# Group statistics taken out of a recurrence's chain, its copies a step later, a new table of a round's pieces, and another split of the query rotation

## The chip, the cores and the metric

The kernel runs on one core of a Trainium2 chip. The metric is device microseconds of one execution. Names of engines: PE is TensorE's matmul, PEld its weight load, DVE is VectorE, ACT is ScalarE, POOL is GpSimd, SP is SyncE.

## The reference, cut to what matters

A first block (convolution and attention, then a feed-forward part) is followed by a two-layer second block over 528 tokens (16 learned ones ahead of 512). Its first layer is a recurrence with 32 heads of 64, its second is an attention with 16 heads. What the change touches is the recurrence with its normalisation over each head's 64 values, and the rotation of the queries:

```python
def _wkv7_scan(r, decay, k, v, a_vec, b_vec):
    ...
    def step(S, inp):
        r_t, w_t, k_t, v_t, a_t, b_t = inp
        sa = jnp.einsum('bhij,bhj->bhi', S, a_t)
        S = S * w_t[:, :, None, :] + sa[..., None] * b_t[:, :, None, :] + v_t[..., None] * k_t[:, :, None, :]
        return S, jnp.einsum('bhij,bhj->bhi', S, r_t)
    ...
    y = _wkv7_scan(r, decay, k, v, -kk, kk * a.astype(jnp.float32))
    mean = jnp.mean(y, axis=-1, keepdims=True)
    var = jnp.mean(jnp.square(y - mean), axis=-1, keepdims=True)
    y = ((y - mean) * lax.rsqrt(var + GN_EPS)).reshape(B, L, D_INNER)

def _rope(x, pos):
    ...
    x1, x2 = xf[..., :half], xf[..., half:]
    return jnp.concatenate([x1 * cos - x2 * sin, x2 * cos + x1 * sin], axis=-1).astype(x.dtype)
```

## The kernel before, in words

All products are made in fp32 from parts: an operand is split into a high part (a copy by ScalarE, `whi`, `qnh`, `knh`) and a low part (a subtraction by GpSimd or VectorE, `wlo`, `qnl`, `knl`), and three matmuls replace one.

The program has three stages: the first block up to about 840 us, the recurrence with the projections that feed it up to about 1900 us, and the attention heads with the output projection to the end.

The recurrence takes the 32 heads in 16 pairs (`Pair`). A pair has 9 chunks (16 tokens, then 8 of 64), and `chain()` takes them one after the other in three steps each. Step one: a bank of PSUM z gets the state's part (L2282) and the mask product's part (L2284), and ScalarE copies it to Z. Step two: z by the inverse R (L2289), and ScalarE's VU. Step three: z by AY and KT (L2294, L2297), from which VectorE makes the next state S (L2301, or L2303 for the first chunk), copies the output to yt or y0 (L1920), and takes the statistics of that output with bn_stats, once for each of the two heads (L2311, L2307). The banks of z are two to a pair and two pairs are in work at once, so a chunk's bank is needed again by the same chain two chunks later, and at a chain's start by the pair after next.

A round begins with a new pair's first z. It holds 15 steps of the new pair and 12 of the old one, in the order MAIN, 27 in all. Between two steps `weave()` pulls pieces of other streams, one piece for a letter, by the table PLAN (L1804, a string of letters for each step): O operands of the pair two ahead, B inverses of its 16 x 16 blocks, L and X the inverse of the pair one ahead and its merge, F rates and K keys of the pair three ahead, M transposes, P the split of weights, R and V loads, and Q `post()` of the pair two behind. Instructions stand on their engine's queue in the order in which they are pulled, so the table sets the order of the work on all engines. All these streams but the keys share one ring of three PSUM banks ("t"), used in turn.

Pieces that the prediction speaks of. Keys: a bank pk of its own with 24 matmuls, pulled two by two (L2009), then a copy kx (L1920). Operands: ScalarE's squares and kk (L1915), GpSimd's kp, the norm n (L2035, L2036) with VectorE's nv, GpSimd's AR (L2052) and kb, VectorE's bd (L2059), kk (L2062) and rk (L2072), a product of two arrays in SBUF; then four groups n of eight matmuls (L2085), each with two VectorE products AN and AY that read its bank (L2089, L2090). Merge: a level y (L2219), then r and t, and so on. Weights: ScalarE's whi in two halves and GpSimd's wlo (L1941). Post: VectorE's short operations on the statistics (L2326 to L2331), GpSimd's power, the normalisation by ScalarE and GpSimd, transposes yT, and a store.

In the heads `Heads` weaves one head's attention with the projections of the next and with parts of the output projection. Evictions of a bank are put down with due times, counted in TensorE's columns (`later`, the table W), and forced when a bank or an operand is needed (`need`, `bank`); the banks "mm" are a ring of three. `p_r` (L1185) rotates the queries of two heads, so it runs eight times. VectorE makes the product with the cosines, rt, from the bank ar, and four products of 32 partitions with the sines, ru, also from ar (L1193), and adds them (L1198); for each head ScalarE makes the high part qr (L1201) and GpSimd the low one (L1202). qnh and qnl (L1172, L1171) empty the bank an of the queries' other part, knh and knl that of the keys, and `last` is a tile of transposed probabilities.

Of the kernel before, what the change touches and what calls it, by code (L numbers as in the profile page):

```python
# [15 lines left out]
P = 128  # L16
S = 512
# [886 lines left out]
SCB = 2  # L904
PTB = 2
LAG = 1.0
ROPE = "dpd"
SCALE = "dpdd"
W = dict(max=2200, exp=100, tot=1400, scale=200, hi=400, lo=150, r0=1700, r1=900, r2=1100, z0=1900, z1=1300)
KS = [0, 16, 144, 272, 400]  # L910
KN = [16, 128, 128, 128, 128]
POF = [0, 144, 416, 816]
# [175 lines left out]
class Heads(Late):  # L1088
# [96 lines left out]
    def p_r(s, h, w):  # L1185

        nc, tp = s.nc, s.tp
        key = ("r", h // 2)
        pp = s.bank("mm", key, MM)
        yield from s.mm3(pp, wv(w, 4, 256)(P), s.CQ)  # L1190
        t1, t2 = (tp.tile([P, S], F32, tag=tg, name=f"{tg}{h}", bufs=1) for tg in ("rt", "ru"))
        c, sn = s.tab[:, 0], s.tab[:, 1]
        pr = lambda o, x, t: nc.vector.scalar_tensor_tensor(o, pp[x], SC, t[x], ALU.mult, ALU.mult)  # L1193
        e = [nc.vector if x == "d" else nc.gpsimd for x in ROPE]
        q4 = [slice(32 * i, 32 * i + 32) for i in range(4)]
        ops = [(0, lambda: pr(t1, slice(None), c))]
        ops += [(0, lambda i=i: pr(t2[q4[i ^ 1]], q4[i], sn)) for i in range(4)]
        ops += [(W["r0"], lambda: e[0].tensor_tensor(t1, t1, t2, ALU.add))]  # L1198
        for b, r in enumerate(HS):
            qr = s.x[h + b, "r"] = tp.tile([P, S], F32R, tag="qr", name=f"qr{h + b}", bufs=4)  # L1200
            ops += [(W["r1"], lambda qr=qr, r=r: nc.scalar.activation(qr[r], t1[r], AF.Copy)),  # L1201
                    (W["r2"], lambda qr=qr, r=r, o=HS[1 - b]: e[1].tensor_tensor(qr[o], t1[r], qr[r].bitcast(F32), ALU.subtract))]  # L1202
        s.later(key, *ops)

    def p_k(s, h, w, i=0):
# [142 lines left out]
    def values(s, h, j):  # L1348
        nc, tp, k = s.nc, s.tp, s.k
        vs, vh, vl = s.v[h // 2]  # L1350
        c = ct(h % 2)
        s.need(("t", h, j), ("v", h | 1, j))
        th, tl = s.pt[j]
        if j == 0:
            s.po = s.bank("po", ("z", h), 1)
            nc.tensor.matmul(s.po, lhsT=vs[:96, c], rhs=th[:96], start=True, stop=False)
            return 512
        a = min((j - 1) * P, 256)
        for i, (x, y) in enumerate(((vh, th), (vl, th), (vh, tl))):
            nc.tensor.matmul(s.po[:, a:], lhsT=x[:, j - 1, c], rhs=y[:, :S - a], start=False, stop=j == 4 and i == 2)  # L1360
        if j == 4:
            s.z[h] = zh, zl = [tp.tile([P, S], F32R, tag="z" + x, name=f"z{x}{h}", bufs=6) for x in "hl"]
            z = tp.tile([P, S], F32, tag="az", name=f"az{h}", bufs=1)
            po = s.po
            s.later(("z", h), (0, lambda: nc.vector.scalar_tensor_tensor(z, po, 0.5, s.sg[h], ALU.mult, ALU.mult)),
                    (W["z0"], lambda: nc.scalar.activation(zh, z, AF.Copy)),
                    (W["z1"], lambda: (nc.vector if ROPE[2] == "d" else nc.gpsimd).tensor_tensor(zl, z, zh.bitcast(F32), ALU.subtract)))
        return 3 * (S - a)


# [430 lines left out]

PLAN = ("OMOKO", "OMOOM", "OOO", "ML", "KO", "OMPOM", "KPO", "OPOO", "OMOKKQ", "XMX", "KOB", "XQK", "QQKO", "XKQKK", "MKXBQX", "KXXOB", "OMBB", "KQXK", "KB", "BVBKF", "XFOQKFQXQ", "KFQXX", "BKXQF", "FKKX", "BFOKBKQ", "RBBFMB", "KKOXBXKB")  # L1804

# [64 lines left out]
class Pair:  # L1872
# [387 lines left out]
    def chain(s):  # L2260
# [5 lines left out]
        for c in range(NC_):  # L2266
# [15 lines left out]
                mm(z[:, :P], lhsT=s.AR[:, c - 1], rhs=S, start=True, stop=False)  # L2282
            for h, q in enumerate(HS):
                mm(z[u, q], lhsT=AK[o, hw[h]] if c else AK[o, h, :], rhs=VU[o, q], start=c == 0 and h == 0, stop=h == 1)  # L2284
            Z = T_("Z" + "ab"[p % 2], (P, P), bufs=2)
            s.ev("Z", Z[u], z[u, :P])
            yield
# [7 lines left out]
            if c < NC_ - 1:  # L2295
                for q in HS:
                    mm(z[q, 2 * P:2 * P + 64], lhsT=KT[:, q], rhs=VU[:, q], start=True, stop=True)  # L2297

                for q in HS:
                    if c:  # L2300
                        nc.vector.scalar_tensor_tensor(Sn[q, q], S[q, q], s.wc[q, c - 1:c], z[q, 2 * P:2 * P + 64], ALU.mult, ALU.add)  # L2301
                    else:
                        nc.vector.tensor_copy(Sn[q, q], z[q, 2 * P:2 * P + 64])  # L2303
            if c == 0:
                s.ev("y0", s.y0, z[:16, :P])
                for h, q in enumerate(HS):
                    nc.vector.bn_stats(s.st[:16, 8 + h, :], z[:16, q])  # L2307
            else:
                s.ev("yt", s.yt[o, j, :], z[o, :P])
                for h, q in enumerate(HS):  # L2310
                    nc.vector.bn_stats(s.st[o, 2 * j + h, :], z[o, q])  # L2311
            yield

    def post(s):
# [8 lines left out]
        var = T_("var", (P, 10))  # L2323
        dm = T_("dm", (P, 10))
        me, mo = st[:, :, 1], st[:, :, 4]
        nc.vector.tensor_tensor(dm, me, mo, ALU.subtract)  # L2326
        nc.vector.tensor_tensor(var, st[:, :, 2], st[:, :, 5], ALU.add)
        nc.vector.tensor_tensor(dm, dm, dm, ALU.mult)
# [60 lines left out]
```

## Time and profile before

| | us |
|---|---|
| median of 3 runs | 2497.18 |
| lowest and highest of them | 2495.27, 2511.31 |
| the profiled execution | 2500.02 |
| its span | 2498.2 |
| TensorE busy in it | 2307.1 |

The rows further down are of that one execution. In a row of a timeline the first number is the start in microseconds, the second the time in the instruction (or in several, with "x4"), and a bracket at its end says how long the engine had stood idle before it and which instruction ended that. A row of waits gives the engine, the line that waited, what it waited for, the sum, the number of times and the longest one. In a row of windows PEclk is TensorE's granted clock as a share of full speed.

### The profile page before, as it was taken

The page shows a single profiled execution, that of the slowest core. Times are in us where ns is not written, and L with a number is a line of the kernel's source. Part 1 is how long each engine was busy: PE and PEld are TensorE (multiplying, and loading weights), DVE is VectorE, ACT ScalarE, POOL GpSimd, SP SyncE. Part 2 cuts the span into 40 slices and gives each one's busy share as a digit, 9 for nine tenths or more (in the row PEclk, how much of TensorE's full clock was granted, in tenths as well). Part 3 has the DMA queues.
Part 4 walks back from the last instruction along what each step waited for, and adds up shares of the span by engine and source line. Part 5 has one row for each costly group of instructions (what it writes and reads, how often), then busy time and mean ns, then how long its engine had stood idle before and what let it go on. Part 6 is the DMA issues. An engine that isn't in the chain of part 4 may idle for free. (4 is left out here: it accounts for less than half of the span.)

```text
span 2498.2 us, 42030 instructions
## 1 busy us (share of the span) xinstructions
PE 2307.1 (92%) x16446; PEld 1976.8 (79%) x16446; DVE 1356.9 (54%) x2956; ACT 991.5 (40%) x2292; POOL 1231.3 (49%) x1431
## 2 busy tenths in 40 slices
PE   7999999999998999898999999999988799999996
PEld 5888888878887999886777777777768587887885
DVE  6762236725746450325677767776333632766665
ACT  5553333423434342222434344444332322554442
POOL 5244555646755663535555455555333634434333
PEclk9999999999998999997999888997889799999998
DMA  3113222223233332322222222223223332111212
GB/s 127 68 68 136 89 97 85 91 92 109 87 112 129 120 120 100 114 97 67 56 59 73 58 63 55 58 64 92 76 67 102 134 110 95 63 65 62 70 52 95
DMA packets 135494, 217.01 MB, mean 87 GB/s; under 512 B 60864, under 2 KB 85888, under 8 KB 125056
## 3 DMA queue, kind: packets, MB, share of 16 engines
q1 hardware_dynamic: 123168, 191.63, 23.7%
q10 hardware_dynamic: 12128, 22.70, 2.4%
q8 instruction: 129, 2.11, 0.3%
q14 instruction: 69, 0.57, 0.1%
HBM read 179.28 MB, written 35.00 MB: 86 GB/s over the span
## 5 line engine op out<-in xcount | busy, mean ns | idle before, releaser
L261 POOL TENSOR_TENSOR wlo<-wraw,whi 128x512 fp32r<-128x512 f32 (+1 forms) x312 | 440.2, 1440 | 333.1 <-ACT whi L260 333.0
L941 POOL TENSOR_TENSOR wlo<-wraw,whi 128x512 fp32r<-128x512 f32 (+2 forms) x207 | 253.9, 1240 | 321.9 <-ACT whi L940 314.3
L260 ACT ACTIVATE whi<-wraw 128x512 fp32r<-128x512 f32 (+1 forms) x312 | 175.3, 615 | 253.3 <-issue 80.4
L940 ACT ACTIVATE whi<-wraw 128x512 fp32r<-128x512 f32 (+2 forms) x207 | 115.3, 590 | 65.5 <-PE p_o_t L1713 20.4
L269 PE MATMUL pu<-f_xh,whi 128*128 128x512 f32 x336 | 131.1, 390 | 0.0
L271 PE MATMUL pu<-f_xh,wlo 128*128 128x512 f32 x336 | 130.7, 389 | 0.0
L270 PE MATMUL pu<-f_xl,whi 128*128 128x512 f32 x336 | 130.7, 389 | 0.0
L1915 ACT ACTIVATE VU<-z,fix_nv 64x64 f32<-64x64 f32 x256 | 64.7, 301 | 161.1 <-PE z L2289 160.4
L2301 DVE SCALAR_TENSOR_TENSOR fix_S<-fix_S,wc,z 64x64 f32<-64x64 f32 x224 | 62.4, 279 | 78.8 <-PE z L2297 45.7
L2009 PE MATMUL pk<-lh_k,whi 128*128 128x264 f32 x256 | 88.1, 344 | 5.6 <-DVE kx L1920 5.6
L2009 PE MATMUL pk<-ll_k,whi 128*128 128x264 f32 x256 | 87.3, 341 | 0.0
L2085 PE MATMUL n<-AR,fix_kb 64*128 64x128 f32 x512 | 74.9, 338 | 13.1 <-DVE AYa L2090 6.8
L1305 POOL COPY ap<-apr 128x96 f32<-128x96 f32 x64 | 16.9, 264 | 141.9 <-DVE apr L1302 102.0
L2009 PE MATMUL pk<-lh_k,wlo 128*128 128x264 f32 x256 | 86.4, 338 | 0.0
L2136 POOL TENSOR_TENSOR t<-n,r 66x14 f32<-66x14 f32 (+6 forms) x224 | 74.0, 330 | 16.2
L2085 PEld LDWEIGHTS n<-AR,fix_kb 64*128 64x128 f32 x512 | 66.9, 236 | 18.3 <-issue 9.4
L1599 PE MATMUL p_g<-lh_g,wlo 128*128 128x264 f32 x256 | 74.9, 292 | 2.6 <-POOL wlo L941 2.5
L2282 PE MATMUL z<-fix_S,AR 128*128 128x128 f32 x256 | 60.3, 321 | 17.6 <-DVE fix_S L2303 11.6
L1599 PE MATMUL p_g<-lh_g,whi 128*128 128x264 f32 x256 | 76.2, 298 | 0.0
L1599 PE MATMUL p_g<-ll_g,whi 128*128 128x264 f32 x256 | 74.3, 290 | 0.0
L816 DVE SCALAR_TENSOR_TENSOR ab<-z,vecs,ab 128x511 f32<-128x511 f32 x44 | 55.6, 1264 | 33.7 <-ACT ab L815 33.7
L270 PEld LDWEIGHTS pu<-f_xl,whi 128*128 128x128 f32 x336 | 63.1, 188 | 13.4 <-issue 0.2
(846 smaller groups left out, 7522.6 us busy)
## 6 DMA issues: line engine op xcount, KB each, us to landing
wraw<-in_w_up_dram SPq DMA_DIRECT2D x22, 1024.0 KB
wraw<-in_w_dn_dram SPq DMA_DIRECT2D x16, 704.0 KB
wraw<-in_a_h_dram SPq DMA_DIRECT2D x16, 640.0 KB
wraw<-in_l_k_dram SPq DMA_DIRECT2D x16, 576.0 KB
wraw<-in_w_gt_dram SPq DMA_DIRECT2D x8, 1024.0 KB
wraw<-in_l_v_dram SPq DMA_DIRECT2D x8, 1024.0 KB
wraw<-in_l_r_dram SPq DMA_DIRECT2D x8, 1024.0 KB
wraw<-in_l_g_dram SPq DMA_DIRECT2D x16, 512.0 KB
```

What stands on the lines that cost most here:

```text
L260: nc.scalar.activation(hi[:p, o], raw[:p, o], AF.Copy)
L261: nc.gpsimd.tensor_tensor(lo[:p, o], raw[:p, o], hi[:p, o].bitcast(F32), ALU.subtract)
L269: nc.tensor.matmul(out, lhsT=wh, rhs=xh, start=start and k == 0, stop=False)
L270: nc.tensor.matmul(out, lhsT=wh, rhs=xl, start=False, stop=False)
L271: nc.tensor.matmul(out, lhsT=wl, rhs=xh, start=False, stop=stop and k == n - 1)
L940: nc.scalar.activation(hi[:, o], raw[:, o], AF.Copy)
L941: nc.gpsimd.tensor_tensor(lo[:, o], raw[:, o], hi[:, o].bitcast(F32), ALU.subtract)
L1599: nc.tensor.matmul(b[:, :HL], lhsT=a, rhs=c[:, o], start=kk == 0 and n == 0, stop=kk == KB - 1 and n == 2)
L1915: s.nc.scalar.activation(out, x, AF.Copy if bias is None else AF.Identity, **({} if scale is None else {"scale": scale}), **({} if bias is ...
L2009: s.nc.tensor.matmul(b_[:, :HL], lhsT=a, rhs=b[:, o], start=i == 0 and q == 0, stop=i == n - 1 and q == 2)
L2085: mm(b_[:, ct((c - 1) % 4)], lhsT=kb[HS[h], c], rhs=s.AR[HS[h], c - 1], start=True, stop=True)
L2136: g.tensor_tensor(tmp[:, :q, :m], n16[:, :q, q:q + 1].to_broadcast([66, q, m]), r16[:, q:q + 1, q + 1:].to_broadcast([66, q, m]), ALU.mult)
```

## The change

The statistics leave `chain()`; `post()` takes them from yt and y0 in SBUF, in five new pieces ahead of its other work, two bn_stats each, on all 128 partitions for the four tiles of yt and on 16 for y0. The copy to yt or y0 of a chunk is put off (`late`) to the next chunk's first step, behind its matmuls; that of the last chunk stays. PLAN gets another order, with 17 Q in place of 13. In `p_r` ScalarE copies the bank ar to rs, scaled; GpSimd makes the product with the cosines and the sum, VectorE the four products with the sines from rs; the due times become other ones. The constant ROPE goes; zl, which it also ruled, stays on VectorE.

```diff
@@ -904,9 +904,8 @@
 SCB = 2
 PTB = 2
 LAG = 1.0
-ROPE = "dpd"
 SCALE = "dpdd"
-W = dict(max=2200, exp=100, tot=1400, scale=200, hi=400, lo=150, r0=1700, r1=900, r2=1100, z0=1900, z1=1300)
+W = dict(max=2200, exp=100, tot=1400, scale=200, hi=400, lo=150, rot=900, z0=1900, z1=1300)
 KS = [0, 16, 144, 272, 400]
 KN = [16, 128, 128, 128, 128]
 POF = [0, 144, 416, 816]
@@ -1188,18 +1187,17 @@
         key = ("r", h // 2)
         pp = s.bank("mm", key, MM)
         yield from s.mm3(pp, wv(w, 4, 256)(P), s.CQ)
-        t1, t2 = (tp.tile([P, S], F32, tag=tg, name=f"{tg}{h}", bufs=1) for tg in ("rt", "ru"))
+        t0, t1, t2 = (tp.tile([P, S], F32, tag=tg, name=f"{tg}{h}", bufs=1) for tg in ("rs", "rt", "ru"))
         c, sn = s.tab[:, 0], s.tab[:, 1]
-        pr = lambda o, x, t: nc.vector.scalar_tensor_tensor(o, pp[x], SC, t[x], ALU.mult, ALU.mult)
-        e = [nc.vector if x == "d" else nc.gpsimd for x in ROPE]
         q4 = [slice(32 * i, 32 * i + 32) for i in range(4)]
-        ops = [(0, lambda: pr(t1, slice(None), c))]
-        ops += [(0, lambda i=i: pr(t2[q4[i ^ 1]], q4[i], sn)) for i in range(4)]
-        ops += [(W["r0"], lambda: e[0].tensor_tensor(t1, t1, t2, ALU.add))]
+        ops = [(W["hi"], lambda: nc.scalar.activation(t0, pp, AF.Copy, scale=SC)),
+               (1500, lambda: nc.gpsimd.tensor_tensor(t1, t0, c, ALU.mult))]
+        ops += [(W["rot"], lambda i=i: nc.vector.tensor_tensor(t2[q4[i ^ 1]], t0[q4[i]], sn[q4[i]], ALU.mult)) for i in range(4)]
+        ops += [(W["rot"], lambda: nc.gpsimd.tensor_tensor(t1, t1, t2, ALU.add))]
         for b, r in enumerate(HS):
             qr = s.x[h + b, "r"] = tp.tile([P, S], F32R, tag="qr", name=f"qr{h + b}", bufs=4)
-            ops += [(W["r1"], lambda qr=qr, r=r: nc.scalar.activation(qr[r], t1[r], AF.Copy)),
-                    (W["r2"], lambda qr=qr, r=r, o=HS[1 - b]: e[1].tensor_tensor(qr[o], t1[r], qr[r].bitcast(F32), ALU.subtract))]
+            ops += [(0 if b else 2500, lambda qr=qr, r=r: nc.scalar.activation(qr[r], t1[r], AF.Copy)),
+                    (1500, lambda qr=qr, r=r, o=HS[1 - b]: nc.gpsimd.tensor_tensor(qr[o], t1[r], qr[r].bitcast(F32), ALU.subtract))]
         s.later(key, *ops)
 
     def p_k(s, h, w, i=0):
@@ -1364,7 +1362,7 @@
             po = s.po
             s.later(("z", h), (0, lambda: nc.vector.scalar_tensor_tensor(z, po, 0.5, s.sg[h], ALU.mult, ALU.mult)),
                     (W["z0"], lambda: nc.scalar.activation(zh, z, AF.Copy)),
-                    (W["z1"], lambda: (nc.vector if ROPE[2] == "d" else nc.gpsimd).tensor_tensor(zl, z, zh.bitcast(F32), ALU.subtract)))
+                    (W["z1"], lambda: nc.vector.tensor_tensor(zl, z, zh.bitcast(F32), ALU.subtract)))
         return 3 * (S - a)
 
 
@@ -1801,7 +1799,7 @@
 
 
 
-PLAN = ("OMOKO", "OMOOM", "OOO", "ML", "KO", "OMPOM", "KPO", "OPOO", "OMOKKQ", "XMX", "KOB", "XQK", "QQKO", "XKQKK", "MKXBQX", "KXXOB", "OMBB", "KQXK", "KB", "BVBKF", "XFOQKFQXQ", "KFQXX", "BKXQF", "FKKX", "BFOKBKQ", "RBBFMB", "KKOXBXKB")
+PLAN = ("OKOMOO", "OMOOM", "OO", "ML", "KQ", "OMPOQ", "KMPOQ", "OPOOXQO", "OMOKKQQ", "M", "XXKOB", "XQK", "QQKO", "XKQKK", "MKXBQX", "KXXOB", "OMKBB", "KQX", "KBB", "BVBKF", "XFOQKFQXQ", "KFQXX", "BKXFKK", "FQ", "BFOKBKQ", "RBBFMB", "KKOXBXKB")
 
 
 
@@ -2282,6 +2280,8 @@
                 mm(z[:, :P], lhsT=s.AR[:, c - 1], rhs=S, start=True, stop=False)
             for h, q in enumerate(HS):
                 mm(z[u, q], lhsT=AK[o, hw[h]] if c else AK[o, h, :], rhs=VU[o, q], start=c == 0 and h == 0, stop=h == 1)
+            if c:
+                late()
             Z = T_("Z" + "ab"[p % 2], (P, P), bufs=2)
             s.ev("Z", Z[u], z[u, :P])
             yield
@@ -2301,14 +2301,13 @@
                         nc.vector.scalar_tensor_tensor(Sn[q, q], S[q, q], s.wc[q, c - 1:c], z[q, 2 * P:2 * P + 64], ALU.mult, ALU.add)
                     else:
                         nc.vector.tensor_copy(Sn[q, q], z[q, 2 * P:2 * P + 64])
+
             if c == 0:
-                s.ev("y0", s.y0, z[:16, :P])
-                for h, q in enumerate(HS):
-                    nc.vector.bn_stats(s.st[:16, 8 + h, :], z[:16, q])
+                late = lambda z=z: s.ev("y0", s.y0, z[:16, :P])
             else:
-                s.ev("yt", s.yt[o, j, :], z[o, :P])
-                for h, q in enumerate(HS):
-                    nc.vector.bn_stats(s.st[o, 2 * j + h, :], z[o, q])
+                late = lambda z=z, o=o, j=j: s.ev("yt", s.yt[o, j, :], z[o, :P])
+            if c == NC_ - 1:
+                late()
             yield
 
     def post(s):
@@ -2323,6 +2322,13 @@
         var = T_("var", (P, 10))
         dm = T_("dm", (P, 10))
         me, mo = st[:, :, 1], st[:, :, 4]
+        for j in range(5):
+            for h, q in enumerate(HS):
+                if j < 4:
+                    nc.vector.bn_stats(st[:, 2 * j + h, :], yt[:, j, q])
+                else:
+                    nc.vector.bn_stats(st[:16, 8 + h, :], s.y0[:, q])
+            yield
         nc.vector.tensor_tensor(dm, me, mo, ALU.subtract)
         nc.vector.tensor_tensor(var, st[:, :, 2], st[:, :, 5], ALU.add)
         nc.vector.tensor_tensor(dm, dm, dm, ALU.mult)
```

The change has two lines fewer ahead of the chain, so a line such as L2301 is the same in both there, while those ahead of it are two lower and those of post six higher.

VectorE in the round of pair 7, from the old pair's yt to the first AN (z_6 and z_7 are the two pairs, bon and rk of pairs 8 and 9, n_9 the groups of pair 9). Before:

```order
L1920 COPY yt_12980<-z_6_13570 64x128
L2311 BN_STATS fix_st_7991<-z_6_13570 64x6 x2
L2201 TENSOR_TENSOR bon_13665<-vP_13419,bo_8_13661 128x264
L2201 TENSOR_TENSOR bon_13665<-vP_13419,bo_8_13662 128x264
L2072 SCALAR_TENSOR_TENSOR rk_13671<-rP_13518,vecs,kp_13494 128x528
L2089 TENSOR_TENSOR AN_13596<-n_9_13685,AN_13596 128x4x64
```

Of the change, from the two bon to the first AN:

```order
L2199 TENSOR_TENSOR bon_13596<-vP_13358,bo_8_13592 128x264
L2199 TENSOR_TENSOR bon_13596<-vP_13358,bo_8_13593 128x264
L2328 BN_STATS fix_st_7993<-yt_12362 128x6 x2
L1918 COPY y_7_13477<-z_7_13478 16x128
L2070 SCALAR_TENSOR_TENSOR rk_13617<-rP_13454,vecs,kp_13436 128x528
L2328 BN_STATS fix_st_7993<-yt_12362 128x6 x2
L1918 COPY yt_12919<-z_6_13511 64x128
L2087 TENSOR_TENSOR AN_13522<-n_9_13630,AN_13522 128x4x64
L2088 TENSOR_TENSOR AYa_13628<-n_9_13630,cst_r 128x4x64
```

Between rk and AN stand now two bn_stats of pair 5 and the old pair's yt copy, and two more bn_stats stand ahead of rk.

TensorE in the same round, the four groups of n_9 and what lies between them (pk of pair 10, y_8 the merge's first level of pair 8). Before:

```order
L2085 MATMUL n_9_13685<-AR_13598,fix_kb_7981 128x128 x4
L2282 MATMUL z_6_13690<-fix_S_7970,AR_11903 128x128
L2284 MATMUL z_6_13690<-VU_12427,AN_11901 64x64 x2
L2085 MATMUL n_9_13698<-AR_13598,fix_kb_7981 128x128 x4
L2085 MATMUL n_9_13705<-AR_13598,fix_kb_7981 128x128 x4
L2085 MATMUL n_9_13712<-AR_13598,fix_kb_7981 128x128 x4
L2289 MATMUL z_7_13673<-Zb_13677,R_13063 64x64 x2
```

Of the change:

```order
L2280 MATMUL z_6_13621<-fix_S_7970,AR_11859 128x128
L2282 MATMUL z_6_13621<-VU_12379,AN_11851 64x64 x2
L2083 MATMUL n_9_13630<-AR_13530,fix_kb_7981 128x128 x4
L2083 MATMUL n_9_13637<-AR_13530,fix_kb_7981 128x128 x4
L2083 MATMUL n_9_13644<-AR_13530,fix_kb_7981 128x128 x4
L2217 MATMUL y_8_13651<-Tm_13562,AN_12965 64x64 x8
L2083 MATMUL n_9_13663<-AR_13530,fix_kb_7981 128x128 x4
L2289 MATMUL z_7_13606<-Zb_13611,R_13003 64x64 x2
```

The old pair's z moved ahead of the first group, and a level y ahead of the fourth.

ScalarE at the fifth rotation (rs, qr of heads 8 and 9, qnh of the bank an, knh of the bank ak). Before:

```order
L1172 ACTIVATE p_6_21988<-at_0_21983 96x512
L940 ACTIVATE whi_21974<-wraw_21710 128x512
L1201 ACTIVATE qr_21994<-rt_21992 64x512
L1201 ACTIVATE qr_21995<-rt_21992 64x512
L1172 ACTIVATE qnh_21996<-an_22000 128x512
L1172 ACTIVATE knh_22026<-ak_1_22028 128x264
L1172 ACTIVATE knh_22026<-ak_0_22037 128x264
```

Of the change:

```order
L1171 ACTIVATE p_6_21868<-at_0_21863 96x512
L939 ACTIVATE whi_21854<-wraw_21590 128x512
L1193 ACTIVATE rs_21872<-ar_21831 128x512
L1171 ACTIVATE qnh_21877<-an_21881 128x512
L1199 ACTIVATE qr_21875<-rt_21873 64x512
L1199 ACTIVATE qr_21876<-rt_21873 64x512
L1171 ACTIVATE knh_21903<-ak_1_21905 128x264
L1171 ACTIVATE knh_21903<-ak_0_21919 128x264
```

qnh stands now ahead of qr, behind rs; knh is still behind qr.

## Rows read from the trace of the kernel before

**Rows 1.** The page's first lines, us busy, share of the span and instructions

```profile
span 2498.2 us, 42030 instructions
PE 2307.1 (92%) x16446; PEld 1976.8 (79%) x16446; DVE 1356.9 (54%) x2956; ACT 991.5 (40%) x2292; POOL 1231.3 (49%) x1431
```

**Rows 2.** Windows, three rounds: us, busy PE PEld DVE ACT POOL, PEclk, DMA share, GB/s

```profile
1408.40:1451.30 42.90, 39.83 (x452) 32.60 (x453) 31.81 (x98) 18.16 (x53) 23.41 (x44) 0.92 0.25 64
1451.30:1499.70 48.40, 45.63 (x452) 37.28 (x453) 31.66 (x98) 18.27 (x53) 23.60 (x45) 0.78 0.26 68
1671.20:1710.50 39.30, 37.17 (x452) 30.30 (x453) 30.30 (x98) 16.79 (x51) 20.77 (x43) 1.00 0.22 55
```

**Rows 3.** Waits of TensorE, 1174 to 1890 us: total, times, longest

```profile
PE z L2282 <- DVE fix_S L2303: 11.6, 12, 1.1
...
PE n L2085 <- DVE AYa L2090: 6.8, 6, 1.1
PE z L2284 <- DVE fix_st L2311: 6.0, 13, 0.5
```

**Rows 4.** Timeline of VectorE, round from 1451.3: start, us, instruction, [idle before]

```profile
1450.76 0.37 DVE L2311 BATCH_NORM_STATS2 fix_st<-z 64x6 f32<-64x64 f32 x2
1451.16 0.43 DVE L1920 COPY kx<-pk 128x264 f32<-128x264 f32 x1
...
1461.63 0.28 DVE L1920 COPY yt<-z 64x128 f32<-64x128 f32 x1
...
1462.90 2.15 DVE L2072 SCALAR_TENSOR_TENSOR rk<-rP,vecs,kp 128x528 f32<-128x528 f32 x1
...
1465.30 0.41 DVE L2090 TENSOR_TENSOR AYa<-n,cst_r 128x256 f32<-128x256 f32 x1
```

**Rows 5.** Timelines of GpSimd and ScalarE in the same round

```profile
1454.04 1.27 POOL L2052 TENSOR_TENSOR AR<-kk,fix_E 128x512 f32<-128x512 f32 x1 [1.05 <-ACT kk L1915]
...
1461.86 2.62 POOL L1941 TENSOR_TENSOR wlo<-wraw,whi 128x1152 fp32r<-128x1152 f32 x1 [2.30 <-ACT whi L1938]
...
1461.10 0.68 ACT L1938 ACTIVATE whi<-wraw 128x576 fp32r<-128x576 f32 x1
```

**Rows 6.** One line's instructions, L2072: min, median, max ns

```profile
L2072 DVE SCALAR_TENSOR_TENSOR rk<-rP,vecs,kp x16: 749/2139/2519, 1011.3 to 1722.7; 128x528 f32<-128x528 f32 x16
```

**Rows 7.** Timeline of TensorE in the same round, the fourth group of n

```profile
1465.86 1.13 PE L2085 MATMUL n<-AR,fix_kb 64*128 64x128 f32 x8 [1.14 <-DVE AYa L2090]
```

**Rows 8.** Waits of TensorE, 1905 to 2460 us

```profile
PE ao L421 <- DVE qnl L1171: 12.4, 5, 3.1
...
PE at L1330 <- DVE last L1169: 4.8, 2, 2.4
...
PE as L1273 <- ACT knh L1172: 2.2, 1, 2.2
```

**Rows 9.** Timelines of four engines, fifth rotation

```profile
2208.45 0.62 ACT L940 ACTIVATE whi<-wraw 128x512 fp32r<-128x512 f32 x1
...
2208.57 2.79 DVE L1193 SCALAR_TENSOR_TENSOR ru<-ar,tabq 32x512 f32<-32x512 f32 x4
...
2207.84 2.61 POOL L941 TENSOR_TENSOR wlo<-wraw,whi 128x512 fp32r<-128x512 f32 x2
...
2212.83 1.28 ACT L1201 ACTIVATE qr<-rt 64x512 fp32r<-64x512 f32 x2 [3.76 <-DVE rt L1198]
...
2215.51 0.50 PE L421 MATMUL ao<-zh,whi 128*128 128x512 f32 x1 [2.19 <-DVE qnl L1171]
```

**Rows 10.** Windows of 3.4 us around that wait, columns as in rows 2

```profile
2209.10:2212.50 3.40, 3.40 (x21) 2.91 (x21) 3.30 (x6) 0.00 (x0) 1.33 (x2) 1.00 0.29 77
...
2215.90:2219.30 3.40, 3.40 (x11) 2.52 (x9) 1.61 (x5) 0.68 (x2) 0.57 (x2) 0.50 0.00 0
```

**Rows 11.** Lines L1193 and L1198: min, median, max ns

```profile
L1193 DVE SCALAR_TENSOR_TENSOR ru<-ar,tabq x32: 679/686/696, 2116.3 to 2391.2; 32x512 f32<-32x512 f32 x32
...
L1198 DVE TENSOR_TENSOR rt<-rt,ru x8: 673/693/694, 2119.2 to 2391.9; 128x512 f32<-128x512 f32 x8
```

## The prediction

> **What bounds the kernel now.** I read the page's list of engines first [rows 1]: TensorE is busy 2307.1 us of the span of 2498.2 us, so at most 191 us of the whole are waits, and all but a part of those lie in stages that this change leaves alone. The change touches two places, and for each I looked at the stage, not at the average.
>
> The first is the recurrence. Seen by windows from one pair's first z to the next one's, a round has the same instructions and nearly the same work each time, but lasts 42.9 us at a granted clock of 0.92, 48.4 at 0.78 and 39.3 at 1.00 [rows 2]. So a good part of a round's length is TensorE's clock, at the lower of its two levels (1.2 against 2.4 GHz) for some stretches, and not a wait. The list of TensorE's waits in this stage is short [rows 3]: 11.6 us in 12 waits on the state S of the new pair's first chunk (L2303), 6.8 us in 6 waits on the mask product AYa (L2090), 6.0 us in 13 waits on bn_stats (L2311), about 1.0, 1.1 and 0.5 us each. All three sit in the first third of a round. Behind them TensorE has no wait on VectorE.
>
> To see why they are there I followed VectorE through that third in the round that begins at 1451.3 [rows 4], with GpSimd and ScalarE beside it [rows 5]. VectorE is the engine that is late: bn_stats, kx, S, yt and rk stand back to back. rk takes 2.15 us there, starting at 1462.90, while GpSimd's wlo runs from 1461.86 to 1464.48; rk ends 0.57 us after wlo. Over all rounds the same rk takes 749 ns at best and 2139 ns at the median [rows 6]. I read this as: a VectorE instruction with two inputs in SBUF waits until a running GpSimd instruction is done. AN and AYa (0.41 us for AYa) stand right behind rk, and TensorE's fourth group of n waits for AYa from 1464.72 to 1465.86 [rows 7]. A bank is freed by AYa, there are three, and so the fourth user of the ring waits, whoever it is.
>
> The second place is the rotation of queries in the heads, eight times. TensorE waits 12.4 us in 5 waits for qnl, 4.8 in 2 for last and 2.2 in 1 for knh [rows 8], 19.4 us in all. In the fifth rotation [rows 9] the four products ru take 2.79 us on VectorE, ScalarE's two qr come behind the sum, and qnl, which frees a bank, is behind qr on ScalarE's queue; TensorE stands 2.19 us, up to 2215.51. After that wait the clock is at 0.50 for 3.4 us: 11 matmuls there against 21 in the 3.4 us ahead of the wait [rows 10]. A dip so costs up to 3.4 x 10/21 = 1.6 us.
>
> **Statistics out of the chain, copies later.** In the chain 18 bn_stats a pair go, 0.37 us for two [rows 4]; 10 come back in post, on 128 partitions. Cost of one on yt in SBUF: the row shows it only on 64 partitions from PSUM; from below I take half, from above the doubled price, and use the same 0.185, since a line's elements, 64, are unchanged. That is 8 x 0.185 = 1.5 us less on VectorE per pair, but VectorE is idle for long stretches later in a round, so only the first third counts.
>
> There the pair of 0.37 at 1450.76 falls away from in front of kx (1451.16). kx feeds ScalarE's kk, for which GpSimd stood idle 1.05 us up to 1454.04 [rows 5]; from there AR, bd, kk, S follow by turns on the two engines. So S should come about 0.33 us earlier, and the wait of 1.0 on S shrinks to about 0.6. TensorE's wait of 0.5 for bn_stats turns into one of about 0.2 for the last yt copy; it is upstream of the S wait and gives nothing more. ScalarE's second whi (1461.10) is behind Z of the same z, so wlo also moves up by 0.33.
>
> Against this: rk is still reached while wlo runs (VectorE gets there some 0.2 us earlier, and would need 1.0), so it still ends 0.57 after wlo, at about 1464.7. Behind it now stand one pair of bn_stats and one yt copy (0.28 at 1461.63) before AN; those two were done in rk's waiting time before, and now they are not. Together 0.37 + 0.28 = 0.65. AYa ends 0.65 - 0.33 = 0.32 us later than before, and TensorE behind it. The old pair's z goes ahead of the first n group, which needs an S that VectorE now has ready earlier, and the y level that goes ahead of the fourth n group is itself the fourth user of the three banks: it waits for the same AYa. So it doesn't fill the hole, it stands behind it, and the fourth n group after it. No matmul is added or dropped.
>
> Per round: from -0.33 (if the pair and the copy hide after all) to +0.65 (if nothing moves up), by the walk +0.32. Over the 12 full rounds: -4 to +8, I take +4. What is late next is the n groups' evictions and then S of the new pair's next chunk; TensorE has y, r and t levels to do before it asks for that.
>
> **New table of pieces.** The keys' pieces in front of kt and the earlier norm only swap matmuls in a stretch where S is what ends the wait; the norm is then itself up against ScalarE's sq. Zero, with -0.2 to +0.2 a round as bounds, from the 0.33 above. More Q pieces add no DMA and no queue.
>
> **Rotation of queries.** Removed per rotation: VectorE's rt, and the sum on VectorE. Added: ScalarE's rs (0.62, as whi of the same shape), GpSimd's product and sum (1.3 each, as its wlo) [rows 9], and ru reads rs and the table, both in SBUF, where before it read PSUM. The form "two inputs in SBUF, 32 partitions" isn't in the trace. Bounds: the old sum L1198 has two SBUF inputs and took 673 to 694 ns, and the old ru, from PSUM, 679 to 696 even while wlo ran [rows 11]; at that rate every wait vanishes, -19.4 us. From the other side rk [rows 6] says that each ru can lose the rest of a GpSimd instruction. L1198 ran with GpSimd idle; rk is the nearest row for what happens here, since in rotation 5 wlo runs from 2207.84 to 2210.45 and the product on GpSimd follows it.
>
> So I walk it with that, 0.70 for a ru: rs stands behind the whi that ends at 2209.07 and is done at about 2209.7; the first ru waits for wlo's end at 2210.45; then GpSimd's product takes its turn, till about 2212.4, and the other three ru end at 2214.5, qnl at 2215.1. qnh is no longer behind qr. TensorE goes on 0.4 us earlier than 2215.51. ScalarE's qr waits for GpSimd's sum till 2215.7, and knh with VectorE's knl is queued behind qr until 2217, with the first ao group's matmuls as cover; without that cover it would cost up to the 1.3 of GpSimd's sum. The same walk gives, as estimates: 0.4 less for rotations four to six each; 1.0 less for the second and third, where last goes ahead of qr; 0.6 more for the last two, where qnl stands behind two later ru; 2.6 more for the first, where knh stays behind qr and qr is later. Sum 2.6 - 2.0 - 1.2 + 1.2 = +0.6. A dip may go in one or two places (1.6 each); I take -2 for the heads, with -19 and +6 as ends.
>
> The Trainium skill, page "SBUF — State Buffer", section "Who interferes with whom", says that a VectorE instruction with two SBUF inputs is locked out for the whole of a GpSimd instruction that reads SBUF, and that one with a single SBUF input is not. That speaks against this change, which turns ru from the second kind into the first. By the rule the heads come to the -2 above, by the durations of L1198 and of the old ru alone to -19; rk's rows agree with the rule.
>
> **Sum.** 2500.0 us (the profiled execution, 1.8 over its span) + 4 - 2 = 2502. That execution stands 2.8 us above the median of the runs, 2497.2, so I forecast 2499. A measurement of this kernel tells 1%, 25 us, from no change.
>
> **Rivals.** First, ru is not locked out: then all of the 19.4 us go, 2500 + 4 - 19.4 - 2.8 = 2482, and with the dips (8 x 1.6) gone too 2469. For it: L1193 and L1198 never took over 0.70. Against: rk.
>
> Second, slower: VectorE's extra 0.65 between rk and AN comes through whole and makes the hole at the n groups 1.8 us instead of 1.14, and each round then pays one more stretch at the lower clock. Price: 12 x 0.65 = 8 and 12 x 1.6 = 19, less 2 in the heads: 2500 + 8 + 19 - 2 - 2.8 = 2522. It decides from the point where the hole in front of the y level gains more than the 0.33 that the start gives. For it: the round with the lowest clock is 5.5 us longer than its neighbour [rows 2], and a dip follows each wait of 2 us in the heads. Against: the rounds have holes of 1.14 already, and still differ in clock.
>
> Third, the stretches at the lower clock fall less often because the S and bn_stats waits shrink: if half of the 12 rounds came from 42.9 down to 39.3 [rows 2], 6 x 3.6 = 22 us less, 2477, and all of them 2456. One round in twelve does so today without any of this.
>
> Fourth, the change does not shift VectorE's work at all in the time that counts, because kk on VectorE is set by GpSimd alone: +0.65 a round without dips, 12 x 0.65 - 2 - 2.8 = 3 over 2500.0, so 2503; this lies inside the first case's range.
>
> **How the numbers follow.** Forecast (with the fourth) 0.62, its own range 2488 to 2510; no lock 0.20, a third of it under 2472; slower with dips 0.10, most of it past 2522; fewer dips 0.08, somewhat over half of it under 2472. Faster by over 1% 0.12, slower 0.08, within 1% 0.80. The range: 2474 to 2515 leaves a tenth on either side.
>
> **What would show it.** Right: the wait of z on bn_stats is gone from the list; S of the first chunk is some 0.3 us earlier from the round's start; rk still near 2.1 us; the y level L2217, not the n group, waits for AYa, by more than 1.14; ru at a mean well over 0.70 where GpSimd runs beside it; the ao waits still there with about 1.8 us. Wrong: ru at 0.69 throughout and no wait for qnl (then the heads were mispriced); rounds of 41 us or less with no wait on AYa (then rk got in front of wlo); rounds over 44 us (then the clock).

## The result, and the profile after

The changed kernel took 2529.51 us in the median of 19 runs (2505.76 to 2592.80), the kernel before 2498.28 in the median of 19 (2491.72 to 2513.11). The ratio is 1.0094, with an interval of 1.007 to 1.0119; like the ratios of the experiments it leaves out runs over 1.5% above the fastest of their kernel, here five of the 19, while the medians take in all runs. Forecast were 2499 in a range of 2474 to 2515. So the change made the kernel slower, by about 0.9%, and its runs differ from each other far more than those of before.

The profiled execution is the fastest of the 19 (2505.76), so it shows less of the loss than the median has. Its page starts with these lines, which answer to [rows 1]:

```profile
span 2504.0 us, 41895 instructions
PE 2309.3 (92%) x16446; PEld 1975.9 (79%) x16446; DVE 1356.5 (54%) x2812; ACT 997.3 (40%) x2300; POOL 1261.8 (50%) x1447
```

TensorE does the same 16446 matmuls in nearly the same busy time, and the whole shows nothing. The windows over four rounds of the recurrence do, as in [rows 2]; the columns are named in the first line:

```profile
core 0: us, PE busy (x) PEld busy (x) DVE busy (x) ACT busy (x) POOL busy (x), PEclk, DMA share, GB/s
1236.20:1278.80 42.60, 39.18 (x451) 32.03 (x451) 31.36 (x90) 18.18 (x53) 23.48 (x44) 0.92 0.20 47
1278.80:1335.40 56.60, 53.32 (x452) 43.68 (x453) 31.49 (x90) 18.43 (x53) 23.99 (x45) 0.63 0.24 63
1501.20:1556.20 55.00, 51.69 (x451) 42.20 (x451) 31.44 (x90) 18.43 (x53) 23.98 (x45) 0.66 0.25 65
1684.10:1722.30 38.20, 36.27 (x451) 29.42 (x451) 29.75 (x90) 16.81 (x51) 20.89 (x43) 1.00 0.23 56
```

At an equal clock a round became shorter: 42.6 us at 0.92 (before 42.9), 38.2 at 1.00 (before 39.3). But two rounds, the second and third rows, last 56.6 and 55.0 us with a mean clock of 0.63 and 0.66, each some 13 us more than the first; the lowest clock of a full round before was 0.78. The kernel lost its time to TensorE's clock and not to waits.

TensorE's waits in this stage, which answer to [rows 3]:

```profile
PE y L2217 <- issue: 20.1, 9, 2.3
...
PE z L2280 <- DVE fix_S L2303: 4.2, 10, 0.6
```

The wait on bn_stats is gone, the one on S fell from 0.97 to 0.42 us each, and the one on AYa has become a wait of the y level, 20.1 us in 9. The profile writes "issue" where it finds no releaser; the timelines of VectorE and TensorE in the round from 1460.1, beside [rows 4] and [rows 7], show which it is:

```profile
1468.26 0.45 DVE L2303 COPY fix_S<-z 64x64 f32<-64x64 f32 x2
...
1471.66 2.24 DVE L2070 SCALAR_TENSOR_TENSOR rk<-rP,vecs,kp 128x528 f32<-128x528 f32 x1
1473.83 0.34 DVE L2328 BATCH_NORM_STATS2 fix_st<-yt 128x6 f32<-128x64 f32 x2
1474.09 0.26 DVE L1918 COPY yt<-z 64x128 f32<-64x128 f32 x1
...
1474.61 0.40 DVE L2088 TENSOR_TENSOR AYa<-n,cst_r 128x256 f32<-128x256 f32 x1
```

```profile
1459.73 0.28 PE L2297 MATMUL z<-VU,KTa 128*64 128x64 f32 x2
...
1468.77 0.49 PE L2280 MATMUL z<-fix_S,AR 128*128 128x128 f32 x2 [0.39 <-DVE fix_S L2303]
...
1470.59 2.26 PE L2083 MATMUL n<-AR,fix_kb 64*128 64x128 f32 x24
1475.12 0.68 PE L2217 MATMUL y<-Tm,AN 64*64 64x64 f32 x16 [2.26 <-issue]
1475.83 1.13 PE L2083 MATMUL n<-AR,fix_kb 64*128 64x128 f32 x8
```

rk still takes 2.24 us, a pair of bn_stats and a yt copy follow, and y starts 0.1 us after AYa's end (1474.61 + 0.40), which frees its bank. The standstill is 2.26 us, where it was 1.14. In an ordinary round like this one it did little harm beyond itself: the clock fell to 0.50 for 3.4 us, 2.3 us after y's start. In the round from 1278.8 it did. Windows of 3.4 us, columns as above:

```profile
1286.30:1289.70 3.40, 3.01 (x21) 2.18 (x20) 3.26 (x11) 1.45 (x4) 1.10 (x3) 1.00 0.49 141
1289.70:1293.10 3.40, 1.85 (x23) 1.66 (x21) 3.40 (x9) 0.00 (x0) 2.34 (x1) 1.00 0.04 16
1293.10:1296.50 3.40, 2.69 (x23) 2.60 (x24) 2.55 (x9) 0.00 (x0) 0.00 (x0) 0.51 0.00 0
1296.50:1299.90 3.40, 3.40 (x21) 2.71 (x19) 2.43 (x7) 0.51 (x2) 0.00 (x0) 0.50 0.31 71
1317.00:1320.40 3.40, 3.40 (x16) 2.34 (x15) 0.50 (x1) 0.55 (x3) 0.00 (x0) 0.50 0.00 0
1344.40:1347.80 3.40, 3.40 (x18) 2.62 (x17) 2.14 (x9) 1.37 (x5) 0.01 (x1) 0.51 0.02 7
1347.80:1351.20 3.40, 3.40 (x35) 2.99 (x34) 2.69 (x11) 1.23 (x3) 1.41 (x1) 1.00 0.00 0
```

The second row holds most of the standstill (1.85 us busy), the third its end. From the third on the clock is 0.50, and it stays there, with TensorE busy for all of the 3.40 us in the three rows that follow, through the rest of the round and 12 us into the next, until 1347.8. In the last two rows 18 matmuls become 35 in the same time.

Nine rounds of this profile have the standstill. In all nine the clock falls within 0.7 us before and 2.5 us after y's start. In seven of them it is back after 3.4 to 10.2 us, in the two long rounds after 54.6 and 51.2 us.

The heads, as in [rows 8], and the four products ru in one line, as in [rows 11]:

```profile
PE ao L421 <- DVE qnl L1170: 11.8, 5, 3.2
...
PE as L1271 <- ACT knh L1171: 6.0, 3, 4.4
...
PE az L1358 <- ACT ph L1171: 2.4, 2, 1.2
...
PE at L1328 <- DVE last L1168: 2.1, 2, 1.0
```

```profile
L1195 DVE TENSOR_TENSOR ru<-rs,tabq x32: 678/732/1687, 2121.9 to 2397.2; 32x512 f32<-32x512 f32 x32
```

The four sums make 22.3 us, where three made 19.4 and none was on ph.

### The profile page after: what moved, and what is told of

The parts are those of the page before. It is cut to its first block, busy times and chain, and to the rows that moved or that the text cites. A ratio compares the mean times of both kernels' runs of the same rounds, so it can differ in the third digit from the quotient of the medians.

```text
span 2504.0 us, 41895 instructions
## 1 busy us (share of the span) xinstructions
PE 2309.3 (92%) x16446; PEld 1975.9 (79%) x16446; DVE 1356.5 (54%) x2812; ACT 997.3 (40%) x2300; POOL 1261.8 (50%) x1447
## 5 line engine op out<-in xcount | busy, mean ns | idle before, releaser
L939 ACT ACTIVATE whi<-wraw 128x512 fp32r<-128x512 f32 (+2 forms) x207 | 115.5, 590 | 63.2 <-PE p_o_t L1711 19.4
L2301 DVE SCALAR_TENSOR_TENSOR fix_S<-fix_S,wc,z 64x64 f32<-64x64 f32 x224 | 62.5, 279 | 83.3 <-PE z L2297 38.1
L2338 POOL TENSOR_TENSOR var<-var,nhalf 128x10 f32<-128x10 f32 x16 | 31.5, 1969 | 85.3 <-DVE var L2337 85.3
L269 PEld LDWEIGHTS pu<-f_xh,whi 128*128 128x128 f32 x336 | 63.1, 188 | 13.3 <-issue 0.2
L271 PEld LDWEIGHTS pu<-f_xh,wlo 128*128 128x128 f32 x336 | 63.1, 188 | 13.2
```

Source lines behind the costliest of these rows:

```text
L269: nc.tensor.matmul(out, lhsT=wh, rhs=xh, start=start and k == 0, stop=False)
L271: nc.tensor.matmul(out, lhsT=wl, rhs=xh, start=False, stop=stop and k == n - 1)
L939: nc.scalar.activation(hi[:, o], raw[:, o], AF.Copy)
```

## The experiments

All medians are in us. The kernel before ran beside each group, with medians of 2506.75 (e1 to e4), 2501.74 (e5 to e8) and 2497.80 (e9 to e12). "Low rounds" are rounds of 49 us and more among those that begin between 1190 and 1700 us in the profiled run. By this count the kernel before has none and the changed one two. e1 and e6 were profiled in runs of 2578.60 and 2567.46.

| run | what differs | median | ratio to before | low rounds |
|---|---|---|---|---|
| e1 | recurrence alone | 2530.96 | 1.0058 (1.0024 to 1.0092) | 6 |
| e2 | rotation alone | 2506.16 | 1.0003 (0.998 to 1.0026) | 0 |
| e3 | before, longer standstill | 2507.44 | 1.0017 (0.9993 to 1.0041) | 2 |
| e4 | changed, rk late | 2455.11 | 0.9803 (0.9773 to 0.9834) | 0 |
| e5 | changed, merge as before | 2487.68 | 0.9938 (0.991 to 0.9966) | 0 |
| e6 | before, merge as changed | 2554.50 | 1.0101 (1.0052 to 1.0149) | 7 |
| e7 | before, rk late | 2539.36 | 1.0145 (1.0099 to 1.0191) | 5 |
| e8 | e1, rk late | 2453.22 | 0.979 (0.9749 to 0.983) | 0 |
| e9 | changed, first y as before | 2494.73 | 0.9969 (0.9942 to 0.9997) | 0 |
| e10 | e5, first y as changed | 2625.53 | none | 5 |
| e11 | e6, rk late | 2553.51 | 1.019 (1.013 to 1.025) | 5 |
| e12 | e5, rk late | 2472.28 | 0.9864 (0.9781 to 0.9948) | 1 |

The two theories at the start: the longer standstill and the clock behind it (one), or the heads (two).

**Which half carries the loss.** e1 is the change with the old `p_r` and its due times, e2 the kernel before with the new ones (the edit is cut to one line):

```diff
 # e1, against the change
-        ops = [(W["hi"], lambda: nc.scalar.activation(t0, pp, AF.Copy, scale=SC)),
+        ops = [(0, lambda: pr(t1, slice(None), c))]
...
 # e2, against before: the other way round
```

> The recurrence's three parts, with the old rotation of queries. Theory one (TensorE stands 2.26 us in front of the first y level where it stood 1.13 in front of the fourth n group, and after that standstill the clock falls and in some rounds stays low for the whole round): this kernel carries the loss: median 2515 to 2535, runs that differ by tens of us, rounds of 41 to 43 us with a few of 50 to 57. Theory two (the heads carry it: TensorE waits 6.0 us for knh where it waited 2.2): this kernel is at 2490 to 2500 with runs within 15 us of each other.

> The rotation of queries alone, in the kernel before. Theory one: 2494 to 2503, runs as close together as those of before; the heads' waits for qnl, knh, last and ph sum to about 22 us where they were 19.4. Theory two: 2515 or more. Third reading (the first prediction's other case, products from SBUF never held up): 2480 or less, which the 732 ns median and 1687 ns maximum of the products in the changed kernel already speak against.

Theory two falls: the rotation changes nothing that can be measured, and the recurrence alone is slower by itself, with runs from 2501.93 to 2637.10. In e2 the heads' waits for qnl, knh, ph and last are 11.7, 6.0, 2.4 and 2.3, as in the changed kernel.

**Is it the length of the standstill?** e3 lengthens it in the order of before (its new tile, `dum`, is left out here); e4 takes it out of the changed kernel:

```diff
 # e3, against before (results not read)
         nc.vector.scalar_tensor_tensor(s.rk, rP, k.v("r_k", p), kp, ALU.mult, ALU.mult)
+        for i in range(6):
+            nc.vector.bn_stats(s.dum[:, i, :], s.rk[:, 64 * i:64 * i + 64])
         yield
 # e4, against the change
-        s.rk = T_("rk")
-        nc.vector.scalar_tensor_tensor(s.rk, rP, k.v("r_k", p), kp, ALU.mult, ALU.mult)
         yield
...
         s.en("sc").tensor_tensor(s.AR, s.AR, s.wc[:, :8].unsqueeze(2).to_broadcast([P, 8, P]), ALU.mult)
+        s.rk = T_("rk")
+        nc.vector.scalar_tensor_tensor(s.rk, rP, k.v("r_k", p), kp, ALU.mult, ALU.mult)
         yield
```

> The kernel before, with six bn_stats on rk put on VectorE between rk and the first AN, whose results nobody reads; they make the standstill in front of the fourth n group some 1.1 us longer and change nothing else. Theory one: the standstill comes to about 2.2 us, rounds at an equal clock are 1.1 us longer (12 x 1.1 = 13 us), and rounds with the clock low throughout appear: median 2515 to 2540, runs spread by 30 us and more. If only the standstill counts and not the clock: 2508 to 2513 with runs within 15 us.

> The changed kernel, with the product rk put behind the scaling of AR, so that it no longer stands ahead of the first AN. Theory one: the standstill in front of the first y level falls from 2.26 to 0.3 us or less, 12 x 2 = 24 us of waits go, the rounds with a low clock throughout go too, and the time is 2460 to 2485, below both kernels, with runs close together. Theory two (the heads): 2500 or more, since the heads are as in the changed kernel. If S of the next chunk becomes late by rk, TensorE waits on L2301 some 0.5 us a round and half the gain is lost.

In e3 TensorE's wait on AYa, and a round at 0.92:

```profile
PE n L2087 <- DVE AYa L2092: 13.2, 9, 2.0
```

```profile
1413.20:1457.10 43.90, 39.90 (x452) 32.72 (x453) 32.71 (x104) 18.18 (x53) 23.54 (x44) 0.92 0.26 67
```

The standstill is 2.0 us in six rounds (the mean of the 9 waits is 1.5) and the round 1.0 longer than the 42.9 of [rows 2], but the median is that of before, and no such spread came. Two rounds of the profile are long, 50.5 and 51.1 us:

```profile
1457.10:1507.60 50.50, 46.88 (x451) 38.23 (x452) 32.57 (x104) 18.30 (x53) 23.68 (x45) 0.76 0.27 66
```

Their long stretch at 0.50, 30.7 us, begins 33 us into the round and not at the standstill; the kernel before has the same in its round of 48.4 us [rows 2], 31 us into it. So theory one was wrong in its first half: a standstill of 2 us is not enough. In e4, on the other hand, the wait on AYa is gone and the clock stays up. Its longest waits, and two of its rounds:

```profile
PE z L2280 <- DVE fix_S L2301: 7.1, 12, 1.6
...
PE z L2280 <- DVE fix_S L2303: 4.6, 11, 0.6
```

```profile
1355.70:1394.00 38.30, 36.53 (x452) 29.52 (x453) 29.83 (x90) 18.19 (x53) 23.64 (x44) 1.00 0.28 72
1470.40:1508.60 38.20, 36.45 (x451) 29.44 (x451) 29.78 (x89) 18.18 (x53) 23.55 (x44) 1.00 0.29 71
```

Eleven rounds in a row last 38.3 us or less, none with a fall of the clock. The wait for the next chunk's S (L2301), by which the expectation saw half the gain lost, did come, some 0.5 us in a round, and the gain stayed. This kernel is faster than both. What the standstill needs beside it to do harm is sought in the table next.

**What stands behind the standstill.** Theory A: the clock falls at the standstill and comes back soon where the n group and the keys follow; the merge's y level, 64 x 64 matmuls, keeps it low. e5 and e6 exchange the merge's letters (of PLAN's 27 entries only those that differ and their neighbours):

```diff
 # e5, against the change
-"OPOOXQO", "OMOKKQQ", "M", "XXKOB"
+"OPOOQO", "OMOKKQQ", "XMX", "KOB"
 # e6, against before
-"OPOO", "OMOKKQ", "XMX", "KOB"
+"OPOXO", "OMOKKQ", "M", "XXKOB"
```

> The changed kernel with the merge's letters X back in their old steps of the table (the first y level behind the keys' matmuls again, not ahead of the fourth n group); all else is as in the changed kernel. The standstill stays, now in front of the fourth n group, at about 2.2 us. Theory A (the clock falls at the standstill, and comes back soon only where dense matmuls follow; the merge's small matmuls moved up to there keep it low): no more rounds low throughout, median 2490 to 2505, runs within 25 us. Theory B (2.26 us of standstill are enough by themselves): as the changed kernel, median 2515 to 2540 with runs spread by 60 us or more.

> The kernel before with only the merge's letters X in their new steps, so that a y level stands ahead of the fourth n group, behind a standstill of 1.13 us as before. Theory A: rounds with a low clock throughout appear, median 2510 to 2540, runs spread by 50 us or more. Theory B: no change against before, 2495 to 2510, since the standstill isn't longer.

Both moved the way theory A said, and further than it said: e5 ended 2 us below its range and e6 14 us above it. In e5 the standstill is as long as in the changed kernel, in front of the fourth n group:

```profile
PE n L2083 <- DVE AYa L2088: 26.0, 12, 2.3
```

and the rounds are ordinary, at 0.96 and 0.92:

```profile
1358.90:1400.10 41.20, 37.73 (x452) 30.82 (x452) 31.26 (x90) 18.08 (x53) 23.58 (x44) 0.96 0.26 67
1400.10:1442.70 42.60, 39.13 (x451) 32.02 (x451) 31.24 (x89) 18.08 (x53) 23.53 (x44) 0.92 0.25 63
```

e9 and e10 move the first y level alone:

```diff
 # e9, against the change
-"OPOOXQO", "OMOKKQQ", "M", "XXKOB"
+"OPOOQO", "OMOKKQQ", "XM", "XXKOB"
 # e10, against the change
-"OPOOXQO", "OMOKKQQ", "M", "XXKOB"
+"OPOOXQO", "OMOKKQQ", "XM", "KOB"
```

> The changed kernel with the first y level alone put back behind the keys' matmuls; y, r and t of the later levels stay where the change put them. If it is the y level right behind the standstill that keeps the clock low: as the kernel with the whole merge put back, 2480 to 2495, no round low throughout. If it is the crowding of the later levels (y, r, t one behind the other, as here even closer): rounds low throughout, 2515 or more.

> The counterpart: the merge's letters in their old steps, but the first y level stays ahead of the fourth n group, behind the standstill. If the y level there is the cause: rounds low throughout, 2515 or more. If it is the crowding: 2480 to 2495.

With that one level moved back the loss is gone (e9, one of its ten runs at 2520.97 and the others below 2500); with that one level moved forward it is larger than in the change (e10, all four runs above 2570). The profiles say the same of each single standstill of 2 us and more. With the n group next, the clock was back after 3.4 or 6.8 us in all 11 of e5, all 8 of e9 and all 6 of e3. With the y level next, it stayed at 0.50 for 51.2 us or more in 2 of 9 (the change) and in 4 of 6 (e10). Two rounds of e10:

```profile
1236.20:1292.40 56.20, 52.90 (x452) 43.33 (x453) 31.31 (x90) 18.30 (x53) 23.83 (x45) 0.64 0.21 50
1292.40:1353.70 61.30, 61.30 (x452) 50.43 (x452) 30.00 (x90) 18.28 (x53) 23.54 (x43) 0.50 0.18 45
```

In the second TensorE is busy for all of 61.30 us, and the clock is 0.50 for the whole round. It isn't waiting for anything; it does the same 452 matmuls at the lower level of its clock.

**Without the standstill.** e7 is the kernel before with rk late, e8 the recurrence alone with rk late, e11 and e12 are e6 and e5 with rk late (the edit of e4 in each).

> The kernel before with rk behind the scaling of AR. Both theories: the standstill of 1.13 us in front of the fourth n group goes, and with it the clock's fall behind it; rounds of 38 to 39 us where they were 41.4 to 42.9, 12 x 4 = 48 us less: 2445 to 2465. If the waits on bn_stats and S (0.5 and 0.95 us) are enough for a fall of the clock, rounds stay at 40 to 42 us and the time is 2480 to 2490.

> The changed recurrence with the old rotation of queries and rk behind the scaling of AR. The heads then wait 19.4 us in place of some 22: 2450 to 2457 against the 2455 of the kernel with the new rotation; a difference of over 10 us either way would say that the rotation isn't neutral once the recurrence doesn't disturb it.

> The kernel before with rk behind the scaling of AR and the merge's letters in their new steps; statistics and copies stay in the chain. If the merge spread over the round and no standstill are what keeps the clock up: rounds of 38.5 to 39.5 us at a full clock, 2455 to 2470; the rest to the 2453 of the changed recurrence with rk late is what the statistics and copies give (the waits on bn_stats 0.49 and the longer one on S, 0.55, a round: 12 us). If the statistics and copies are needed for a steady clock: 2490 or more.

> The changed kernel with rk late and the merge's letters in their old steps. As in the kernel before with rk late, no standstill ahead of the two y levels one behind the other: if these and not the statistics made that kernel slow, the clock falls some 20 us into a round and stays low into the next: 2500 to 2530. If the statistics' place matters more: 2465 or less.

e8 agrees with e4, but for one of its four runs at 2522.21: the rotation is neutral there too. e7 and e11 missed: without any wait on AYa they are slower than before. A round of each at a full clock is short, 39.8 and 39.7, but others stay low:

```profile
1238.30:1290.30 52.00, 49.55 (x452) 40.26 (x453) 30.27 (x98) 18.41 (x53) 23.54 (x44) 0.70 0.22 54
1429.40:1469.20 39.80, 37.03 (x451) 29.98 (x452) 30.24 (x98) 18.20 (x53) 23.46 (x44) 1.00 0.28 71
```

```profile
1243.20:1300.70 57.50, 55.90 (x452) 45.78 (x453) 30.55 (x98) 18.51 (x53) 23.43 (x44) 0.60 0.20 49
1350.00:1389.70 39.70, 37.44 (x452) 30.29 (x453) 30.36 (x98) 18.29 (x53) 23.47 (x44) 1.00 0.29 74
```

e11's waits in the first third are those of before:

```profile
PE z L2282 <- DVE fix_S L2303: 8.7, 9, 1.1
PE z L2284 <- DVE fix_st L2311: 4.3, 10, 0.5
```

There the clock falls some 11 us into a round, behind these waits and with the y level next; in e4 the same stretch has 0.42 us for S and none for bn_stats, and no fall. e7 has a wait that the kernel before has not, for the next chunk's S, ahead of which rk now stands on VectorE:

```profile
PE z L2282 <- DVE fix_S L2301: 6.1, 9, 1.0
```

Behind three of these nine waits, by 2.0 to 2.4 us, the clock falls for 44.4 us, some 20 us into the round; the merge's r and t levels, matmuls of 64 x 64 and 32 x 32, stand right behind them. e12 lies between, as two of its four runs are at 2456 and 2458 and two at 2487 and 2499. Ordered by three things, the medians are:

| | merge as before | merge as changed |
|---|---|---|
| rk as before, statistics in the chain | 2498 | 2554 (e6) |
| rk as before, statistics in post | 2488 (e5) | 2530 (the change) |
| rk late, statistics in the chain | 2539 (e7) | 2554 (e11) |
| rk late, statistics in post | 2472 (e12) | 2455 (e4) |

"Statistics in post" stands for the statistics, the late copies, and the new places of the keys and the norm together; these were not tried apart. The place of the merge's letters decides where rk is as before: 56 and 42 us in the medians, 25 and 39 by the ratios. With rk late it does not: 14 us one way and 17 the other, with intervals that overlap.

## Why the prediction was wrong

**The step that failed** is the one on the new table, "Zero, with -0.2 to +0.2 a round as bounds", and with it the sentence on the y level: "So it doesn't fill the hole, it stands behind it, and the fourth n group after it." The order was read rightly: y waits for AYa, as the fourth user of the ring. But I priced what stands behind a standstill at nothing, since no matmul is added. e5 against the change is 42 us in the medians, for the merge's letters alone, and e9 gives 35 of them back by one level; by the ratios to the kernel before beside each it is 39 and 31 us. The rise is a few rounds in which the clock stays at 0.50 from the standstill to the round's end, some 13 us each.

**Statistics and copies.** I took +4 us. Most pieces of the walk hold: the bn_stats wait gone, S at 0.42 where I said about 0.6, rk still held, the pair and the copy behind it. But the standstill of 2.26 does not come from a later AYa. In the kernel before, in the round from 1451.3, this row ends 0.49 us before its first z:

```profile
1450.50 0.28 PE L2297 MATMUL z<-VU,KTa 128*64 128x64 f32 x2
```

I count from its end, and in the changed kernel from the end of the same row at 1459.73. S starts after 8.62 us in the kernel before and after 8.25 now, 0.37 earlier where I said 0.33. (From the round's start, by which I meant to see it, it is 8.13 and 8.14, as the round itself now begins without a wait.) AYa ends after 14.93 and 15.00, only 0.07 later where I said 0.32. TensorE stands from 13.94 and 12.85 on: it reaches the same AYa 1.1 us earlier, since it no longer stands the 0.49 for bn_stats and 0.55 of the 0.94 for S. So the short waits were gathered into one, about 3 us in all either way. The sum had the wrong sign: with the merge as before, the statistics, copies and the rest of the table together are a gain (e5, 0.9938, some 15 us). Which of them makes it was not tried; in the profiles, before, one round lasted 48.4 us, and in e5 none is over 42.7 us.

**Rotation.** I took -2 us with the products held up by GpSimd; e2 shows no difference (-5 to +6.5 us by its interval). In the fifth rotation the walk gave 2214.5 - 2209.7 = 4.8 us for four ru and a wait of about 1.8. VectorE there, and TensorE's next ao:

```profile
2221.15 4.49 DVE L1195 TENSOR_TENSOR ru<-rs,tabq 32x512 f32<-32x512 f32 x4 [0.32 <-ACT rs L1193]
2225.68 0.69 DVE L1170 SCALAR_TENSOR_TENSOR qnl<-an,qnh 128x512 fp32r<-128x512 f32 x1
...
2226.42 0.50 PE L421 MATMUL ao<-zh,whi 128*128 128x512 f32 x1 [1.81 <-DVE qnl L1170]
```

4.49 us in place of 2.79 [rows 9], and 1.81 us, as walked. The line's median is 732 ns and its maximum 1687, where it was 686 and 696. The Trainium skill, page "SBUF — State Buffer", section "Who interferes with whom", has a VectorE instruction with two SBUF inputs shut out while GpSimd reads SBUF; the trace agrees, with the 1687 ns.

**Rivals.** The second rival came nearest: it said 2522, with the clock as its price, and had a chance of 0.10. Its reason, a longer standstill in each round, is not the one: e5 has the longer standstill in 11 of its 12 rounds, e3 in six, and neither loses by it. (Its "a dip follows each wait of 2 us in the heads" holds but for one: behind the 2.38 us that end at 2149.41 the clock stays at 1.00.) It is not one more short stretch a round but few long ones, and they come by what follows. That the measured time lies near its 2522 is luck. The first rival (no lock) is refuted by ru's row; the third did come true, but only in e4 and e8, where rk is late.

**Open.** Why the clock came back soon in seven of the changed kernel's nine rounds and not in the other two, with the same instructions, the trace does not tell. That it is the small size of the y level's matmuls that keeps the clock low, as theory A has it, was not tried apart from their place. And e7 and e11 show that long stretches at 0.50 come without the standstill at the n groups too; six of e7's nine waits for the next chunk's S have none behind them, so that wait alone is not the reason either.

## What to carry to other kernels

Where TensorE is at work nearly all the time, ask not only how long it stands at a wait, but what it does next: what stands right behind a standstill, here a level of small matmuls, can cost more than the standstill (e9, e10). Read a stage's windows with the granted clock round by round before and after; means and busy shares of the whole hid two rounds of 55 us. A product that nobody needs soon (rk) belongs behind the evictions that free a bank: that alone, on top of this change, took the kernel from 2530 to 2455 us. But the same edit in the kernel before made it slower, 2502 to 2539 us (e7), for a reason that stays open; so such a move has to be measured in the order in which it is to run.

## What the runs showed of the hardware

TensorE's clock can stay at 0.50 through a whole round of 61.30 us in which the profile shows the engine no idle time (e10). The Trainium skill, page "TensorE: Matmul & The Clock Gate", Part 1, says that "activity releases the throttle"; here an engine that the profile calls busy throughout was not released for 116.1 us. In another order of the same matmuls, with no wait over 0.6 us, the clock stayed at 1.00 for eleven rounds (e4).

A fall of the clock went with every standstill of 2.0 to 2.3 us in the recurrence: in all 40 of them (9 in the change, 6 in e3, 11 in e5, 8 in e9, 6 in e10) it came between 0.7 us before and 2.5 us after the end. In the heads of the kernel before one of 2.38 us, up to 2149.41, had none behind it.
